# Entry of an FFN kernel: input loaded per column range into all partitions, interleaved with the first weights by quarters, norm scales applied in the split into two parts

## The chip, the cores and the metric

One core of one Trainium2 chip. The metric is the device time of one execution in microseconds (us). The kernel before was timed in three runs: 1007.42, 1010.66 and 1010.75 us, median 1010.66.

## The reference, cut to what matters

A trunk of two layers on an input x of 256 rows by 1024 columns, all float32. Each layer is `h += 0.5 * ffn(h)`, `h += mixer(h)`, `h += 0.5 * ffn(h)`; the mixer of layer 0 is a diagonal state-space layer (S5), that of layer 1 is block-sparse attention (MoBA).

```python
def rms_norm(x, g):
    y = x * lax.rsqrt(jnp.mean(x * x, axis=-1, keepdims=True) + EPS)
    return y * g

def swiglu(h, w_gate, w_up, w_down):           # h: rms_norm(h, g), 1024 columns; D_FF = 2816
    return (jax.nn.silu(h @ w_gate) * (h @ w_up)) @ w_down
```

Only the first FFN's beginning (layer 0) is touched by the change: x comes from memory, is normalised with the scales g of the first norm, and is multiplied with the gate and up weights.

## The kernel before, in words

**Phases.** `phases` is f00, s5, f01, f10, moba, f11, one after the other. The rows of h lie as two row tiles t = 0, 1 of 128 partitions each (`h2`, 128 x 2 x 1024).

**Products in two parts.** Every operand is cut into a high and a low part in the type fp32r, and a product is three matmuls (`mm3`, L385): high x high (L386), high x low weights (L387), low x high weights (L388). For a weight half of 128 x 1024, `Stream.split` (L72) lets ScalarE (ACT) copy it to whi (L81) and VectorE (DVE) subtract to wlo (L82). For x the tile `xa` holds both parts, transposed: `X["h"]` and `X["l"]`, 128 x 8 x 256, where k = 0 to 7 counts blocks of 128 columns.

**Weights.** They come in units of 1 MB in a fixed order, each with three raw buffers (RAW = 3), so the first three units are asked for when `Stream` is made. For the FFN's block j of 256 hidden columns there are two gate/up units a = 0, 1 (512 rows of w each, gate and up side by side), loaded by `ld_gu` (L161). Block 0 is loaded in steps of two k, so each of its four halves ("quarters" of the sum over 1024) is two transfers of 256 KB, one of gate and one of up. All of them are issued on SyncE's (SP) queue. `st.pump()` splits the next half if a slot is free; `st.get` splits it at the latest when it is needed. A raw buffer is asked for anew when both halves of its unit have been split.

**The order.** Every engine's instructions stand in the order in which the Python code issues them; there is no scheduler behind it. `fill` (L1304) counts estimated time and brings forward pieces of the S5 tables (the generator `tables`, L607, whose next piece is run by `next(tab, None)`) between the FFN's products.

**The entry** (L1311 to L1370):
- `ld_x(0)` (L247) loads the columns 0 to 511 of x by four transfers of 128 KB to 32 partitions each. The list `ahead` holds `ld_x(1)`, the other half, which the first call of `ld_gu` with a = 1 issues, so it stands between the second and the third pair of weight transfers.
- `busy(12)` (L1328): 12 products of `ones` with themselves, 24 matmul instructions in the profile, since a float32 product is two of them. `gains()` (L273) transposes the norm scales `gn` on TensorE (PE) and copies them to `gT`.
- `pre(t, n)` (L1311): four transposes of row tile t's columns of half n on PE (L1319), and a DVE multiply by gT in PSUM (L1320). `parts(t, n)` (L1323): ACT copies to the high part (L1325), DVE subtracts to the low part (L1326). `square` (L1339): ACT sums squares of x for the norm.
- Order: `pre` for both t of half 0, `parts` of t = 0, `busy(6)` with table pieces around it, split, `parts` of t = 1, split, two squares. `second` (L1343) does the same for half 1, and then the norm's factors on GpSimd (POOL; `rsq`, L292) and the loading of ACT's Silu table (`warm`, L226). It is a hook that runs ahead of the products q = 1, t = 0.

**gu0** (L446), the FFN's block 0: for the quarters q = 0 to 3, for t = 0, 1, two k of three matmuls, 48 in all, into the PSUM banks `psA(0)` and `psA(2)`. `hooks` holds functions to be run ahead of a pair (q, t). Then `gated` (L466) for each t: ACT computes sg, the Silu of the gate times the norm factor (L468), DVE act = up times factor times sg (L472); then `st.pump(2)`. The next block, `gu(1, 0)` (L428), has 24 matmuls for t = 0 with the transposes of act (`tr`, L474) ahead of k = 3 and k = 6. From there on the FFN goes on in this manner, with the down products between.

Of the kernel before, what the change touches and what calls it, by code (L numbers as in the profile page):

```python
# [10 lines left out]
F32 = mybir.dt.float32  # L11
F32R = mybir.dt.float32r
AF = mybir.ActivationFunctionType
OP = mybir.AluOpType
AX = mybir.AxisListType

D = 1024
# [98 lines left out]
def trunk_kernel(ctx: ExitStack, tc, x, ffn_norm, ffn_w_gate, ffn_w_up, ffn_w_down, mix_norm,  # L116
# [3 lines left out]
    nc = tc.nc  # L120
# [13 lines left out]
    def psR():  # L134
        return pp.tile([128, 512], F32, name="pR", tag="R", bufs=2)

    def psA(i):
        return pp.tile([128, 512], F32, name=f"pA{i}", tag=f"A{i}", bufs=1)
# [20 lines left out]
    ahead = []  # L159

    def ld_gu(l, i, j, a, step=4):  # L161
        def f(t):
            v = t.rearrange("p (k c) -> p k c", c=512)
            cs = slice(j * 256, (j + 1) * 256)
            if ahead and a:
                ahead.pop()()
            for k in range(0, 4, step):
                r = slice(a * 512 + k * 128, a * 512 + (k + step) * 128)
                for o, w in ((0, ffn_w_gate), (256, ffn_w_up)):
                    nc.sync.dma_start(v[:, k:k + step, o:o + 256],  # L170
                                      w[l, i, r, cs].rearrange("(k p) c -> p k c", p=128))
        return f
# [53 lines left out]
    def warm(func):  # L226

        w = sp.tile([128, 1], F32, name="warm", tag="warm", bufs=1)
        nc.scalar.activation(w, ones[:, 0:1], func)

    cst = cp.tile([128, 320], F32, name="cst")
    ident = cst[:, 0:128]
# [6 lines left out]
    h2 = cp.tile([128, 2, D], F32, name="h2")  # L239
    h = [h2[:, t, :] for t in range(2)]  # L240

    def rows(t, s, n):

        tiles = [[128 * D, 2]] if t is None else []
        return [((t or 0) * 128 + s) * D + n * 512, [[4 * D, 32]] + tiles + [[1, 512]]]

    def ld_x(n):  # L247
        for s in range(4):
            off, ap = rows(None, s, n)
            nc.sync.dma_start(h2[s * 32:s * 32 + 32, :, n * 512:(n + 1) * 512],  # L250
                              bass.AP(tensor=x.tensor, offset=x.offset + off, ap=ap))

    nc.scalar.dma_start(gn, ffn_norm.rearrange("l i (k p) -> (l i k) p", p=128))
    ld_x(0)
    warm(AF.Exp)
    ahead.append(lambda: ld_x(1))
    if "s5" in phases:
        rho = cp.tile([128, 32], F32, name="rho")
        tstack, lstack, xstack = ExitStack(), ExitStack(), ExitStack()
# [2 lines left out]
        ldt = tabp.tile([32, 2], F32, name="ldt")  # L262
# [5 lines left out]
    st = Stream(nc, units, rp, hp)  # L268

    gT = cp.tile([128, 48], F32, name="gT")  # L270
    st.gT = gT

    def gains():  # L273
        ps = psR()
        nc.tensor.transpose(ps[:, 0:32], gn, ident[0:32, 0:32])
        nc.vector.tensor_copy(gT[:, 0:32], ps[:, 0:32])
# [11 lines left out]
    X = {}  # L288
# [3 lines left out]
    def rsq(o, v, n):  # L292

        e = sp.tile([128, n], F32, name="rs_e", tag=f"rs_e{n}", bufs=2)
        nc.gpsimd.tensor_tensor(o, v, nhalf[:, 0:n], op=OP.pow)  # L295
        nc.gpsimd.tensor_tensor(e, o, o, op=OP.mult)
        nc.gpsimd.tensor_tensor(e, e, v, op=OP.mult)
        nc.gpsimd.tensor_scalar(e, e, -0.5, 1.5, op0=OP.mult, op1=OP.add)
        nc.gpsimd.tensor_tensor(o, o, e, op=OP.mult)
# [6 lines left out]
    def home(pool, ph):  # L306

        xa = pool.tile([128, 4224], F32R, name="xa")
        v = xa[:, XO[ph]:XO[ph] + 4096].rearrange("p (i k c) -> p i k c", i=2, c=256)
        return v[:, 0], v[:, 1]  # L310
# [51 lines left out]
    def boundary(nxt, parts, acc, scale, mid=None):  # L362

        if nxt is not None and nxt[0] == "f":
            order = [(0, 0), (1, 0), (0, 1), (1, 1)]
        else:
            order = [(0, 0), (0, 1), (1, 0), (1, 1)]
        for i in range(2):
            for part in parts[:-1]:
                part(*order[i])  # L370
            if mid is not None and i == 0:
                mid()
        for i, (t, n) in enumerate(order):
            for part in parts[-1:] if i < 2 else parts:
                part(t, n)
            finish(t, n, acc[2 * t + n], scale)
            if nxt is None:
                store(t, n)
            elif i:
                prep(*order[i - 1], nxt)  # L380
# [226 lines left out]
    def tables(tp):  # L607

        V, P = nc.vector, nc.gpsimd

        def T(name, *shape):
            return tp.tile([128] + list(shape), F32, name=name)
# [17 lines left out]
        for m in MPs + [TT] + t3s:  # L630
            P.memset(m, 0.0)
        yield
        dts = tp.tile([32, 2], F32, name="dts")
        nc.scalar.activation(dts, ldt, AF.Exp)
        dtb = tp.tile([32, 2, 64], F32, name="dtb")
        V.tensor_copy(dtb, dts[:, :, None].to_broadcast([32, 2, 64]))
        yield
        ps = psR()
        nc.tensor.transpose(ps[:, 0:32], scn[:, 0, :], ident[0:32, 0:32])
# [18 lines left out]
        ps = psR()  # L658
# [38 lines left out]
        q, y, y2, e0, e1, den = (T(n, 32) for n in ("q", "y", "y2", "e0", "e1", "den"))  # L697
# [213 lines left out]
        while work or later or dma:  # L911
# [8 lines left out]
            while work and work[0][1] <= now and credit >= work[0][0] and done[0] >= work[0][4]:  # L920
# [3 lines left out]
                t = max([now + LAG] + [a[0] + PACE for a in later])  # L924
# [365 lines left out]


    tab = tables(tabp) if "s5" in phases else iter(())
    next(tab, None)
    slot = [0]
# [13 lines left out]
        while extra and slot[0] > extra[0][0]:  # L1308
            extra.pop(0)[1]()

    def pre(t, n):  # L1311

        if not X:
            X[phases[0], "x"] = True
            X["h"], X["l"] = home(XP[0], phases[0])
        ps = psA(2 * t + n)
        pv = ps.rearrange("p (k c) -> p k c", c=128)
        for k in range(4):
            nc.tensor.transpose(pv[:, k, :], h[t][:, n * 512 + k * 128:n * 512 + (k + 1) * 128], ident)  # L1319
        nc.vector.tensor_tensor(pv, pv, gT[:, n * 4:n * 4 + 4, None].to_broadcast([128, 4, 128]), op=OP.mult)  # L1320
        return pv

    def parts(t, n, pv):  # L1323
        xh, xl = (X[p][:, n * 4:n * 4 + 4, t * 128:t * 128 + 128] for p in "hl")
        nc.scalar.activation(xh, pv, AF.Copy)  # L1325
        nc.vector.tensor_tensor(xl, pv, xh.bitcast(F32), op=OP.subtract)  # L1326

    def busy(n):  # L1328

        ps = psR()  # L1330
        for _ in range(n):
            mm(ps[:, 0:128], ones, ones, start=True, stop=True)

    busy(12)
    gains()
    next(tab, None)
    ss4 = sp.tile([128, 2, 2], F32, name="ss4", tag="ss4", bufs=1)

    def square(t, n):  # L1339
        sq = sp.tile([128, 512], mybir.dt.bfloat16, name="sq", tag="sq", bufs=1)  # L1340
        nc.scalar.activation(sq, h[t][:, n * 512:(n + 1) * 512], AF.Square, accum_out=ss4[:, t, n:n + 1])

    def second():  # L1343

        pv = [pre(t, 1) for t in range(2)]
        for t in range(2):
            parts(t, 1, pv[t])
        st.pump()
        for t in range(2):
            square(t, 1)  # L1350
        v2, r2 = (sp.tile([128, 2], F32, name=n, tag=n, bufs=1) for n in ("ms2", "rr2"))
        nc.gpsimd.tensor_tensor(v2, ss4[:, :, 0], ss4[:, :, 1], op=OP.add)
        nc.gpsimd.tensor_scalar(v2, v2, 1.0 / D, EPS, op0=OP.mult, op1=OP.add)
        rsq(r2, v2, 2)
        for t in range(2):
            Rr[t] = r2[:, t:t + 1]
        st.pump()
        warm(AF.Silu)

    pv = [pre(t, 0) for t in range(2)]  # L1360
    parts(0, 0, pv[0])
    next(tab, None)
    busy(6)
    st.pump()
    next(tab, None)
    parts(1, 0, pv[1])
    st.pump()
    for t in range(2):
        square(t, 0)
    first = {(1, 0): [second]}  # L1370

    for i, ph in enumerate(phases):
        nxt = phases[i + 1] if i + 1 < len(phases) else None
# [59 lines left out]
```

## Time and profile before

| | |
|---|---|
| profiled execution, device time | 1010.79 us |
| its span (first to last instruction) | 1009.0 us |
| outside the span | 1.79 us |
| mean granted clock of TensorE | 0.994 |
| bytes read from memory, written | 182.84 MB, 13.66 MB |
| DMA, mean over the span | 196 GB/s |

The profile is one execution of the program, with times in us from the span's start. In the rows of the timeline stand start, duration, engine, line and operation, then the tile written and the tiles read, the shapes, the count of instructions put together in the row ("x8"), and in brackets how long the engine sat idle before it and what ended that wait. PE is TensorE's matmuls, PEld its weight loads, SPq SyncE's queue of DMA issues. A row of the windows has, after the window's length, the busy time of PE, PEld, DVE, ACT and POOL with counts, then the granted clock of TensorE as a share of full speed, the mean busy share of the 16 DMA engines, and GB/s. A row of a DMA queue has packets, MB, and the time its packets took as a share of 16 engines' time in that window.

### The profile page before, as it was taken

How to read it: one execution, taken by the hardware profiler on the slowest of the kernel's cores; microseconds unless marked ns; L12 is line 12 of the kernel's file. 1: busy time of each engine (PE TensorE's matmuls, PEld its weight loads, DVE VectorE, ACT ScalarE, POOL GpSimd, SP SyncE). 2: the span in 40 equal slices, each digit the busy share in tenths (PEclk: the TensorE clock that was granted, in tenths of full speed). 3: DMA queues.
4: the chain of work that ended last, by engine and by line, in shares of the span. 5: the costliest groups of instructions: out<-in, count | busy, mean ns of one | idle time of the engine just before them, and what ended most of it. 6: DMA issues, size and time to landing. Idle time of an engine off the chain costs nothing.

```text
span 1009.0 us, 16573 instructions
## 1 busy us (share of the span) xinstructions
PE 996.0 (99%) x6394; PEld 892.6 (88%) x6394; DVE 704.6 (70%) x1145; ACT 574.8 (57%) x1040; POOL 165.3 (16%) x330
## 2 busy tenths in 40 slices
PE   8999999999999999999999999999999999999998
PEld 7788888888998899999989999999888899999997
DVE  4799666857968677666657766666689667766662
ACT  5566777754236556555546555553788665555551
POOL 4971222113740100000010000000342010000000
PEclk9999999999899999999999999999999999999999
DMA  8896776886736557565626765655354456656531
GB/s 249 216 295 208 253 259 210 264 317 232 260 115 189 196 186 237 167 209 168 208 85 209 236 222 170 208 168 172 116 168 139 156 174 210 221 197 206 171 125 43
DMA packets 137535, 197.59 MB, mean 196 GB/s; under 512 B 16288, under 2 KB 109040, under 8 KB 137200
## 3 DMA queue, kind: packets, MB, share of 16 engines
q1 hardware_dynamic: 133264, 183.27, 56.7%
q0 software_dynamic: 3616, 12.66, 3.2%
q8 instruction: 50, 0.82, 0.3%
q10 hardware_dynamic: 576, 0.61, 0.2%
q14 instruction: 29, 0.24, 0.1%
HBM read 182.84 MB, written 13.66 MB: 195 GB/s over the span
## 4 chain that ended last, share of the span: by engine, by line
PE 91%; DVE 3%; issue 2%; POOL 2%; ACT 1%; DMA 0%; SPq 0%; ACTq 0%; POOLq 0%; DVEq 0%
PE pM L541 12%; PE pM L540 12%; PE pM L542 12%; PE pA L387 9%; PE pA L386 9%; PE pA L388 9%; PE pM L386 5%; PE pM L387 5%; PE pM L388 5%; PE pR L322 1%; DVE wlo L82 1%; POOL qrs L295 1%; PE pR L872 1%; PE pR L1035 1%; PE pR L1034 1%
## 5 line engine op out<-in xcount | busy, mean ns | idle before, releaser
L540 PE MATMUL pM<-xa,whi 128*128 128x256 f32 x1056 | 295.7, 280 | 0.0
L541 PE MATMUL pM<-xa,whi 128*128 128x256 f32 x1056 | 294.9, 279 | 0.0
L542 PE MATMUL pM<-xa,wlo 128*128 128x256 f32 x1056 | 294.7, 279 | 0.0
L88 DVE SCALAR_TENSOR_TENSOR wlo<-raw,gT,whi 128x512 fp32r<-128x512 f32 x328 | 228.0, 748 | 70.2 <-ACT whi L87 70.0
L82 DVE TENSOR_TENSOR wlo<-raw,whi 128x1024 fp32r<-128x1024 f32 x156 | 190.7, 1237 | 55.2 <-ACT whi L81 54.0
L87 ACT ACTIVATE whi<-raw,gT 128x512 fp32r<-128x512 f32 x328 | 213.5, 711 | 19.2 <-PE pA L388 14.1
L541 PEld LDWEIGHTS pM<-xa,whi 128*128 128x128 f32 x1056 | 198.5, 188 | 2.6
L540 PEld LDWEIGHTS pM<-xa,whi 128*128 128x128 f32 x1056 | 198.5, 188 | 2.3
L542 PEld LDWEIGHTS pM<-xa,wlo 128*128 128x128 f32 x1056 | 198.5, 188 | 0.0
L81 ACT ACTIVATE whi<-raw 128x1024 fp32r<-128x1024 f32 x156 | 160.8, 1054 | 21.9 <-PE pM L541 6.3
L386 PE MATMUL pA<-whi,ah 128*128 128x512 f32 x352 | 138.8, 394 | 0.0
L387 PE MATMUL pA<-wlo,ah 128*128 128x512 f32 x352 | 137.7, 391 | 0.0
L388 PE MATMUL pA<-whi,al 128*128 128x512 f32 x352 | 137.7, 391 | 0.0
L555 ACT ACTIVATE sg<-gr 128x256 f32<-128x256 f32 x66 | 27.6, 418 | 165.5 <-DVE gr L552 165.5
L386 PE MATMUL pM<-whi,xa 128*128 128x512 f32 x288 | 120.0, 417 | 1.5 <-ACT whi L81 1.5
L387 PE MATMUL pM<-wlo,xa 128*128 128x512 f32 x288 | 113.5, 394 | 0.9 <-DVE wlo L82 0.9
L388 PE MATMUL pM<-whi,xa 128*128 128x512 f32 x288 | 113.5, 394 | 0.0
L337 POOL TENSOR_TENSOR ms<-ss 128x1 f32<-128x1 f32 x10 | 1.9, 194 | 475.9 <-ACT sq L334 475.9
L388 PEld LDWEIGHTS pA<-whi,al 128*128 128x128 f32 x352 | 66.1, 188 | 14.4
L386 PEld LDWEIGHTS pA<-whi,ah 128*128 128x128 f32 x352 | 66.2, 188 | 11.6
L387 PEld LDWEIGHTS pA<-wlo,ah 128*128 128x128 f32 x352 | 66.2, 188 | 11.3
L552 DVE TENSOR_TENSOR gr<-pM,rrow 128x512 f32<-128x512 f32 x66 | 45.5, 689 | 40.6 <-PE pM L542 40.4
(253 smaller groups left out, 1289.6 us busy)
## 6 DMA issues: line engine op xcount, KB each, us to landing
raw<-in_ffn_w_down_dram SPq DMA_DIRECT2D x44, 1024.0 KB, 5.5
raw<-in_ffn_w_gate_dram SPq DMA_DIRECT2D x80, 512.0 KB, 4.0
raw<-in_ffn_w_up_dram SPq DMA_DIRECT2D x80, 512.0 KB, 5.1
raw<-in_moba_w_qkv_dram SPq DMA_DIRECT2D x12, 1024.0 KB, 5.2
TB<-dB SPq DMA_DIRECT2D x8, 768.0 KB, 5.9
raw<-in_ffn_w_gate_dram SPq DMA_DIRECT2D x16, 256.0 KB, 4.4
raw<-in_ffn_w_up_dram SPq DMA_DIRECT2D x16, 256.0 KB, 4.6
dB<-tt POOLq DMA_DIRECT2D x16, 256.0 KB, 5.2
```

The source lines that it names most:

```text
L81: nc.scalar.activation(hi, r, AF.Copy)
L82: nc.vector.tensor_tensor(lo, r, hi.bitcast(F32), op=OP.subtract)
L87: nc.scalar.activation(hi[:, c], r[:, c], AF.Identity, scale=g)
L88: nc.vector.scalar_tensor_tensor(lo[:, c], r[:, c], g, hi[:, c].bitcast(F32), op0=OP.mult, op1=OP.subtract)
L386: mm(o, xh, wh, start=start, stop=False)
L387: mm(o, xh, wl, start=False, stop=False)
L388: mm(o, xl, wh, start=False, stop=stop)
L540: mm(o, a, xh, start=k == 0 and i == 0, stop=False, skip_group_check=True)
L541: mm(o, a, xl, start=False, stop=False, skip_group_check=True)
L542: mm(o, b, xh, start=False, stop=k == 7, skip_group_check=True)
L552: V.tensor_tensor(gr, ps.rearrange("p (i c) -> p i c", i=2), Rr["row"][:, None, :].to_broadcast([128, 2, 256]), op=OP.mult)
L555: nc.scalar.activation(sg, gr[:, 0, :], AF.Silu)
```

## The change

- **Transfers of x.** `ld_x(c, n)` loads n columns from column c by two transfers, one for each row tile, each to all 128 partitions. The source's access pattern is 4 runs of 32 rows (`[[D, 4], [4 * D, 32], [1, n]]`), where before's was 32 rows, then 2 tiles, then the columns; partition 32s + i holds row 4i + s as before. x comes in three pieces: columns 0 to 255, 256 to 511 and 512 to 1023.
- **Interleaving.** `ld_gu` now takes the next entry of `ahead` at each step of two k. SP's order is: x's first quarter, first weights, x's second quarter, second weights, x's half, third weights, fourth weights.
- **Scales in the parts.** `quarter(q)` takes the place of `pre` and `parts`: four transposes (two k, both t) into one PSUM bank (1 or 3), and for each k an ACT operation 128x256 that multiplies by gT while it writes the high part, and a DVE operation that multiplies and subtracts for the low part. The DVE multiplies in PSUM go. In the built program the second ACT operation of a quarter waits for the first DVE operation.
- **Order.** `busy(8)` and `busy(3)` in place of 12 and 6. Each quarter has a hook of its own; the third quarter's transposes stand on PE ahead of the second quarter's 12 products, as the hook (1, 0) holds them, and the fourth's ahead of the third's. The norm's factors and the Silu table come in hook (2, 0). The hooks (3, 0) and (3, 1) each split one more half, so the first unit of block 1 is split before the sg.
- **Tables.** The exponential `dtb` is one ACT operation that reads its input broadcast; before, ACT wrote `dts` and DVE copied it to `dtb` (L636).

```diff
@@ ld_gu
-            if ahead and a:
-                ahead.pop()()
             for k in range(0, 4, step):
+                if ahead:
+                    ahead.pop(0)()
@@ ld_x
-    def ld_x(n):
-        for s in range(4):
-            off, ap = rows(None, s, n)
-            nc.sync.dma_start(h2[s * 32:s * 32 + 32, :, n * 512:(n + 1) * 512],
-                              bass.AP(tensor=x.tensor, offset=x.offset + off, ap=ap))
+    def ld_x(c, n):
+        for t in range(2):
+            nc.sync.dma_start(h2[:, t, c:c + n],
+                              bass.AP(tensor=x.tensor, offset=x.offset + t * 128 * D + c,
+                                      ap=[[D, 4], [4 * D, 32], [1, n]]))
...
-    ld_x(0)
+    ld_x(0, 256)
     warm(AF.Exp)
-    ahead.append(lambda: ld_x(1))
+    ahead.extend([lambda: None, lambda: ld_x(256, 256), lambda: ld_x(512, 512)])
@@ tables
-        dts = tp.tile([32, 2], F32, name="dts")
-        nc.scalar.activation(dts, ldt, AF.Exp)
         dtb = tp.tile([32, 2, 64], F32, name="dtb")
-        V.tensor_copy(dtb, dts[:, :, None].to_broadcast([32, 2, 64]))
+        nc.scalar.activation(dtb, ldt[:, :, None].to_broadcast([32, 2, 64]), AF.Exp)
@@ entry
-    def pre(t, n):
...
-    def parts(t, n, pv):
...
+    def quarter(q):
...
+        ps = psA(1 + 2 * (q % 2))
+        pv = ps.rearrange("p (k c) -> p k c", c=256)
+        for k in range(2):
+            for t in range(2):
+                c = (2 * q + k) * 128
+                nc.tensor.transpose(pv[:, k, t * 128:(t + 1) * 128], h[t][:, c:c + 128], ident)
+        for k in range(2):
+            g = gT[:, 2 * q + k:2 * q + k + 1]
+            xh, xl = (X[p][:, 2 * q + k, :] for p in "hl")
+            nc.scalar.activation(xh, pv[:, k, :], AF.Identity, scale=g)
+            nc.vector.scalar_tensor_tensor(xl, pv[:, k, :], g, xh.bitcast(F32), op0=OP.mult, op1=OP.subtract)
...
-    def second():
...
+    def factors():
...
+    busy(8)
+    gains()
     next(tab, None)
+    quarter(0)
+    busy(3)
     st.pump()
-    next(tab, None)
-    parts(1, 0, pv[1])
-    st.pump()
-    for t in range(2):
-        square(t, 0)
-    first = {(1, 0): [second]}
+    square(0, 0)
+    first = {(0, 1): [lambda: next(tab, None), st.pump, lambda: quarter(1), lambda: square(1, 0)],
+             (1, 0): [lambda: next(tab, None), lambda: quarter(2), st.pump, lambda: square(0, 1)],
+             (2, 0): [lambda: quarter(3), st.pump, lambda: square(1, 1), factors],
+             (3, 0): [st.pump], (3, 1): [st.pump]}
```

More of the change, by code (lines that the diff above doesn't have):

```diff
@@ L1315, in pre @@
             X["h"], X["l"] = home(XP[0], phases[0])
[L1316 to L1321, printed above, removed]
-    def parts(t, n, pv):
-        xh, xl = (X[p][:, n * 4:n * 4 + 4, t * 128:t * 128 + 128] for p in "hl")
-        nc.scalar.activation(xh, pv, AF.Copy)
-        nc.vector.tensor_tensor(xl, pv, xh.bitcast(F32), op=OP.subtract)
+        ps = psA(1 + 2 * (q % 2))
[9 more added lines that the diff above has]
+            nc.vector.scalar_tensor_tensor(xl, pv[:, k, :], g, xh.bitcast(F32), op0=OP.mult, op1=OP.subtract)
     def busy(n):
@@ L1332, in busy @@
             mm(ps[:, 0:128], ones, ones, start=True, stop=True)
-    busy(12)
-    gains()
-    next(tab, None)
     ss4 = sp.tile([128, 2, 2], F32, name="ss4", tag="ss4", bufs=1)
@@ L1341, in square @@
         nc.scalar.activation(sq, h[t][:, n * 512:(n + 1) * 512], AF.Square, accum_out=ss4[:, t, n:n + 1])
-    def second():
-        pv = [pre(t, 1) for t in range(2)]
-        for t in range(2):
-            parts(t, 1, pv[t])
-        st.pump()
-        for t in range(2):
-            square(t, 1)
+    def factors():
         v2, r2 = (sp.tile([128, 2], F32, name=n, tag=n, bufs=1) for n in ("ms2", "rr2"))
@@ L1356, in second @@
             Rr[t] = r2[:, t:t + 1]
-        st.pump()
         warm(AF.Silu)
-    pv = [pre(t, 0) for t in range(2)]
-    parts(0, 0, pv[0])
+    busy(8)
+    gains()
     next(tab, None)
-    busy(6)
+    quarter(0)
+    busy(3)
     st.pump()
-    next(tab, None)
-    parts(1, 0, pv[1])
-    st.pump()
-    for t in range(2):
-        square(t, 0)
-    first = {(1, 0): [second]}
+    square(0, 0)
[3 more added lines that the diff above has]
+             (3, 0): [st.pump], (3, 1): [st.pump]}
     for i, ph in enumerate(phases):
```

## The prediction

> **What bounds the kernel now.** I read the page first (busy times, then the chain that ended last), then the timeline of the first 36 us, where the whole change lies, then windows of the same time for the clock, and last the DMA views.
>
> ```profile
> span 1009.0 us, 16573 instructions
> PE 996.0 (99%) x6394; PEld 892.6 (88%) x6394; DVE 704.6 (70%) x1145; ACT 574.8 (57%) x1040; POOL 165.3 (16%) x330
> PE 91%; DVE 3%; issue 2%; POOL 2%; ACT 1%; DMA 0%; SPq 0%; ACTq 0%; POOLq 0%; DVEq 0%
> ```
>
> PE is busy for 99% and has 91% of the chain. After the entry little is to be had, and what the change earns must be a wait or slow clock of PE at the start. The timeline of the entry:
>
> ```profile
> 0.98 5.49 PE L1332 MATMUL pR<-ones 128*128 128x128 f32 x24 [0.98 <-POOL ones L224]
> 6.40 0.31 PE L275 MATMUL pR<-cst,gn 32*128 32x32 f32 x1
> 6.64 1.28 PE L1319 MATMUL pA<-cst,h 128*128 128x128 f32 x8
> 7.52 1.44 DVE L1320 TENSOR_TENSOR pA<-pA,gT 128x512 f32<-128x512 f32 x2
> 8.40 0.60 ACT L1325 ACTIVATE xa<-pA 128x512 fp32r<-128x512 f32 x1 [3.60 <-DVE pA L1320]
> 8.90 1.05 ACT L81 ACTIVATE whi<-raw 128x1024 fp32r<-128x1024 f32 x1
> 9.03 0.69 DVE L1326 TENSOR_TENSOR xa<-pA,xa 128x512 fp32r<-128x512 f32 x1
> 10.00 0.49 PE L386 MATMUL pA<-whi,xa 128*128 128x512 f32 x1 [0.24 <-DVE gm L646]
> 10.03 1.22 DVE L82 TENSOR_TENSOR wlo<-raw,whi 128x1024 fp32r<-128x1024 f32 x1
> 11.31 0.50 PE L387 MATMUL pA<-wlo,xa 128*128 128x512 f32 x1 [0.82 <-DVE wlo L82]
> ```
>
> The order is: warm-up products, scales, transposes of x, multiply, high part, then the weights' whi and wlo. The first product that matters is the second one, at 11.31, when wlo is there. 48 products make gu0; the last begins at 24.29. What follows it is the other loss:
>
> ```profile
> 24.29 0.40 PE L388 MATMUL pA<-whi,xa 128*128 128x512 f32 x1
> 24.73 0.48 ACT L468 ACTIVATE sg<-pA,rr 128x256 f32<-128x256 f32 x1 [0.84 <-PE pA L388]
> 25.10 2.94 ACT L81 ACTIVATE whi<-raw 128x1024 fp32r<-128x1024 f32 x3
> 25.24 0.48 DVE L472 SCALAR_TENSOR_TENSOR act<-pA,rr,sg 128x256 f32<-128x256 f32 x1 [0.83 <-ACT sg L468]
> 26.20 0.50 PE L386 MATMUL pM<-whi,xa 128*128 128x512 f32 x1 [1.51 <-ACT whi L81]
> 27.46 0.74 PE L387 MATMUL pM<-wlo,xa 128*128 128x512 f32 x1 [0.76 <-DVE wlo L82]
> 28.43 0.63 PE L386 MATMUL pM<-whi,xa 128*128 128x512 f32 x1
> 28.85 0.63 PE L387 MATMUL pM<-wlo,xa 128*128 128x512 f32 x1
> 34.84 0.39 PE L387 MATMUL pM<-wlo,xa 128*128 128x512 f32 x1
> 35.07 0.39 PE L388 MATMUL pM<-whi,xa 128*128 128x512 f32 x1
> ```
>
> gu(1,0) waits 1.51 for whi and 0.76 for wlo, since nobody splits its weights before the two sg. Then its products stand 0.42 apart (28.43, 28.85), where later ones stand 0.23 apart (34.84, 35.07). The windows tell why:
>
> ```profile
> 24.37:27.78 3.41, 1.14 (x4) 0.51 (x3) 2.12 (x4) 3.05 (x4) 2.90 (x7) 0.97 0.98 207
> 27.79:31.20 3.41, 3.41 (x11) 2.54 (x10) 2.03 (x2) 0.25 (x1) 3.04 (x5) 0.54 0.31 72
> 31.20:34.61 3.41, 3.25 (x16) 2.43 (x15) 2.27 (x3) 2.66 (x4) 3.00 (x6) 1.00 0.89 255
> 35.10:110.00 74.90, 74.90 (x361) 61.06 (x360) 66.72 (x100) 46.67 (x72) 39.23 (x74) 1.00 0.84 258
> ```
>
> The columns are PE, PEld, DVE, ACT and POOL busy, then the granted clock. In a 3.41-us stretch PE was busy 1.14 us, and the next stretch ran at a clock of 0.54. Such a stretch delays work by half its length, 1.7 us. From 35.1 on PE is busy without a gap. So I measure the change by when gu(1,0)'s last product begins: 35.07 now, 10.8 after gu0's last.
>
> **The change, part by part.** *The new chain per quarter of x.* A quarter has 4 transposes, then ACT high, DVE low, ACT high, DVE low; in the built order the second high stands behind the first low, so these run one after the other. The nearest rows for a 128x256 piece are the sg (0.48) and act (0.48) above, the bounds half of the 128x512 rows (0.30 and 0.35) and those rows whole (0.60 and 0.69); I take 0.48, the same shape. The first weights are split behind the second high: 4 transposes 0.64 (half of 1.28), three pieces 1.45, whi 1.05, wlo 1.22, with 0.1 for handing over: 4.4 us from x's first quarter to the second product. Gone are the DVE multiplies, 0.72 each (1.44/2).
>
> *Fewer warm-up products* (8 in place of 12): 24 instructions take 5.49, 16 take 3.66, so PE comes to the scales at 4.64 and not at 6.40. The 3 in place of 6 further on stand ahead of products that wait for whi anyway; cost nothing either way. The merged dtb saves DVE a piece beside x's chain, worth nothing on PE.
>
> *Two more splits ahead.* The hooks (3,0) and (3,1) pump gu(1,0)'s first two halves while gu0's last quarter runs. Then 1.51 + 0.76 of wait go, and with them the slow stretch. What is late next is the second unit's halves, whose whi must stand behind the two sg: 0.96 and 1.05, and wlo behind the two act, until 3.2 us after gu0's last; 12 products are 12 x 0.227 = 2.7 of that, so 0.5 remains as a wait, and the last half costs 0.3 to 0.6 more. 24 products are 5.45, two pairs of transposes (tr) 0.3: with those waits **6.8** in place of 10.8.
>
> *Squares and factors* are spread over the hooks. The rows of before:
>
> ```profile
> 17.38 0.62 ACT L1341 ACTIVATE sq<-h 128x512 bf16<-128x512 f32 x1
> ...
> 18.92 0.19 POOL L1352 TENSOR_TENSOR ms<-ss 128x2 f32<-128x2 f32 x1 [10.94 <-ACT sq L1341]
> ...
> 19.81 1.28 ACT L229 ACT_TABLE_LOAD   x1
> ...
> 21.74 0.20 POOL L299 TENSOR_TENSOR rr<-rr,rs_e 128x2 f32<-128x2 f32 x1
> ```
>
> Four squares as before, but the last one, the table load (1.28, with 0.2 for the warm-up behind it) and POOL's 3.0 us (18.92 to 21.94) now come in hook (2,0), behind the fourth weights' whi and ahead of the first extra split. They are covered by the 24 products of gu0's second half (5.45), as long as those aren't early; if that cover is gone, the first sg waits for POOL and gu(1,0)'s first wlo for the table, 0.4 us by the times below, which lies inside the waits counted above.
>
> *SP* issues two transfers less before the fourth weights (6 of x for 8, 0.42 each), and the first weights stand behind two x transfers, not four; they aren't on the path, as whi's row names no DMA. From 35 us on the b and c tables' loads go one place later among the weights, beside a queue with time to spare; nothing.
>
> *The transfers.* These decide. The DMA view of x's line, then of three windows (weights in 1-KB packets, 1.8 us; a later phase's 2-KB packets, 1.8 us; x beside other transfers, 2.6 us):
>
> ```profile
> L250 SPq DMA_DIRECT2D h<-in_x_dram x8: 378/425/467, 0.7 to 6.0; - x8
> ...
> DMA to landing us min/median/max: 2.6/4.9/6.8
> ```
>
> ```profile
> q1 hardware_dynamic: 576, 0.61, 103.7%
> ```
>
> ```profile
> q1 hardware_dynamic: 312, 0.61, 87.1%
> ```
>
> ```profile
> q1 hardware_dynamic: 344, 0.53, 71.6%
> ```
>
> MB over window, 16 engines and share give 20.4, 24.3 and 17.8 GB/s for one engine. The first x landed at 0.73 + 2.6 = 3.33; at 16 engines its 128 KB take 0.4, so bytes begin at 2.94.
>
> The new x transfers name 4 runs of 32 rows in their source; before's named 32, the weights 128, and all these kept 16 engines busy. No row has a transfer with an outermost 4. Bounds: it is spread like the others (x at 326 GB/s), or by its outermost count over 4 engines, 4 x 20.4 = 82 GB/s in 1-KB packets and 4 x 24.3 = 97 GB/s in 2-KB ones. I take the second, since the outermost count is just what the rows that used 16 engines do not share with it, and keep both ends.
>
> The Trainium skill, DMA: Bandwidth & Descriptors, section "Why a DMA increments its semaphore by 16 and not by 1", speaks against the change: a transfer runs on the largest number of engines up to 16 that divides the slowest dimension of both its patterns, which is 4 here. Before's rows agree for 32 and 128, and none shows a 4. By it the sum is 1011.0, without it 1008.0 (below).
>
> By 4 engines: 128 KB take 1.6, 256 KB 2.7, and 256 KB of weights on all engines 0.8. One queue in its order gives: x's first quarter 6.1, first weights 7.6, second quarter 10.8, second weights 12.3, x's half 17.7, third weights 19.3, fourth 20.8. Then, by the pieces above:
> - second product 6.1 + 4.3 = 10.4 (now 11.31), and t = 0's others at half clock, since PE had little to do for four us: 12.5. Then the tables' and second quarter's transposes and t = 1's six products, to 15.7.
> - Third quarter's transposes are queued on PE ahead of second quarter's 12 products, and all of these wait for x's half: 2 us, to 18.0. Transposes 0.6, products 2.7: 21.3.
> - whi of the third weights begins behind x's high parts at 20.1; wlo ends at 22.4. So third quarter's second product is at 22.5, and its end at 25.0. The fourth likewise: its transposes run at 21.3, four pieces to 24, wlo 25.8, its end **28.5**, against 24.5 now: +4.0.
> - gu(1,0) 6.8 in place of 10.8: -4.0.
>
> Sum: 0. If a slow stretch falls in the 2-us wait it costs 0 to 1.7, of which wlo's 22.4 and 25.8, which PE's clock does not move, hide most: +0.2. On the profiled execution's 1010.79 (span 1009.0 and 1.79 around it), which lies 0.13 above the median, **1011.0**. Own range 1009 to 1013.5: 6.8 could be 5.8 and the hand-overs 0.8 shorter; the slow stretch could cost its full 1.7 and x's half come 1 us later.
>
> *After 35 us* PE, DVE, ACT and POOL do the same in the same order, with splits up to one place ahead until about 45 us. Two splits less for DVE in a stretch where it is busy 66.72 of 74.90 can only help; I count nothing.
>
> **The rivals.**
> - *x's transfers are spread over all 16 engines.* For it: every transfer seen here is. Against it: the outermost 4. x's first quarter lands with the scales at 4.3; scales' transpose and copy to 5.1, then 4.4: second product 9.5, 1.8 sooner. But PE, whose warm-up now ends at 4.64, stands mostly idle to 9.4, so that a slow stretch follows (1.7), and gu0 ends at about 24.5 as now. Then 6.8 in place of 10.8: -4.0. I let DVE's little room behind it (8.2 us in 75) eat 1.2, as the splits that were ahead are used up: **1008.0**, 1006 to 1009.5.
> - *Slower: x's packets move at the third window's 17.8 GB/s, on 4 engines.* For it: that row is x's own. Against it: few x packets in it had company for long. Then 71 GB/s: 1.85 and 3.7 a transfer and 1.6 for a pair of weights. x's half lands at 2.94 + 3.7 + 1.6 + 3.7 + 1.6 + 7.4 = 20.9, 3.2 later, and the rest moves with it; the wait on PE, now 5 us, surely brings a slow stretch, 1.7: 1011.0 + 3.2 + 1.7 = **1015.9**. It decides once x's half lands after 20, where the wait is longer than a 3.41-us stretch.
> - That the change doesn't do what it says is the forecast itself: all 128 partitions are reached, through a quarter of the engines.
>
> **How the numbers follow.** Forecast 0.52, 16 engines 0.34, slower 0.12; 0.02 for less than 1005.6 by a luckier clock. The runs shown differ by 3.3 (1007.42 to 1010.75), about what one slow stretch or two make, and each case's range holds that. From 1006.0 to 1014.5 lie all but the tails and the slower rival. About 0.5% (5 us) is what a measurement of this kernel can tell from no change: faster (below 1005.6) 0.06, the 0.02 and the lower tail of 16 engines; slower (above 1015.7) 0.07, half the slower rival and the forecast's tail; same 0.87.
>
> **What would show it.** In the changed profile: x's line from issue to landing (the half at about 17.7, or before 12); the mean DMA share while x moves (near 0.3 with 4 engines, near 1 with 16); a wait of PE in L387 or the transposes ending at x's half; second product at 10.4 or 9.5; gu0's last at 28.3 or 24.4; no wait for whi after it; gu(1,0)'s last at 35.1 or 31.3. The forecast is wrong if the half lands late without a later end of gu0, or if gu(1,0) takes far from 6.8.

## The result, and the profile after

The changed kernel takes **1020.08 us** (median of 4 runs, 1017.18 to 1025.85) against 1010.70 beside it: ratio 1.011, 95% interval 1.0082 to 1.0138. It is slower by about 1%, above the range of 1009 to 1013.5. The profiled execution took 1022.31, 11.5 more than that of before. Its page (span, busy time of each engine, chain by engine, chain by line):

```profile
span 1020.5 us, 16539 instructions
PE 1000.8 (98%) x6380; PEld 894.8 (88%) x6380; DVE 702.3 (69%) x1144; ACT 576.4 (56%) x1044; POOL 164.8 (16%) x330
PE 84%; POOL 5%; DVE 4%; issue 3%; DMA 2%; ACT 1%; SPq 0%; POOLq 0%; DVEq 0%; ACTq 0%
PE pM L541 12%; PE pM L542 12%; PE pM L543 12%; PE pA L387 9%; PE pA L389 9%; PE pA L388 9%; PE pM L387 4%; PE pM L389 4%; PE pM L388 4%; DMA h<-in_x_dram 2%; DVE wlo L82 1%; PE pR L323 1%; POOL qrs L296 1%; PE pR L871 1%; PE pR L1033 1%
```

PE is busy for 4.8 us more (1000.8 for 996.0), part of the 11.5; the rest is waiting. Two things weigh more in the chain than before: x's transfer with 2% (0% before), and POOL with 5% (2% before). What PE waited for in the first 50 us (total, times, longest), and the timeline's rows around it:

```profile
PE pA L1320 <- DMA h<-in_x_dram: 4.1, 2, 2.2
PE pA L387 <- ACT whi L81: 1.3, 1, 1.3
PE pR L1331 <- POOL ones L224: 1.0, 1, 1.0
PE pA L388 <- DVE wlo L82: 1.0, 2, 0.5
PE pM L388 <- DVE wlo L82: 0.6, 1, 0.6
```

```profile
7.53 0.90 PE L1320 MATMUL pA<-cst,h 128*128 128x128 f32 x3 [1.90 <-DMA h<-in_x_dram]
...
12.23 0.80 PE L388 MATMUL pA<-wlo,xa 128*128 128x512 f32 x1 [0.46 <-DVE wlo L82]
...
20.39 0.78 PE L1320 MATMUL pA<-cst,h 128*128 128x128 f32 x3 [2.16 <-DMA h<-in_x_dram]
...
31.95 0.39 PE L389 MATMUL pA<-whi,xa 128*128 128x512 f32 x1
...
39.39 0.39 PE L389 MATMUL pM<-whi,xa 128*128 128x512 f32 x1
```

x's first quarter was there at 7.5, its half at 20.4. gu0's last product begins at 31.95 (24.29 before), gu(1,0)'s last at 39.39 (35.07). So the entry alone is 4.3 late, not 11.5. The next 6 are lost where nothing was expected, between 56 and 82 us:

```profile
61.80 0.44 PE L486 MATMUL pR<-cst,act 128*128 128x128 f32 x2 [1.02 <-DVE act L473]
77.30 0.63 PE L811 MATMUL pR<-cst,cn 128*64 128x128 f32 x4 [2.95 <-DVE al L489]
```

```profile
74.00:77.30 3.30, 0.36 (x2) 0.00 (x0) 3.30 (x7) 0.19 (x1) 3.30 (x7) 1.00 0.52 151
77.30:80.70 3.40, 3.40 (x13) 2.55 (x13) 2.50 (x5) 0.75 (x2) 2.61 (x7) 0.69 1.04 357
80.70:84.10 3.40, 3.40 (x13) 2.58 (x13) 2.06 (x4) 1.90 (x2) 0.00 (x0) 0.81 0.60 252
```

In the windows (PE, PEld, DVE, ACT, POOL busy, then clock) VectorE is busy for the whole 3.30 us in which PE does 0.36, and then PE's clock is 0.69 and 0.81. Upstream of it stand two rows of the timeline:

```profile
28.91 0.62 POOL L1341 TENSOR_TENSOR ms<-ss 128x2 f32<-128x2 f32 x1 [20.94 <-ACT sq L1337]
```

```profile
55.54 0.23 DVE L677 COPY e<-c 128x16 f32<-128x16 f32 x1 [2.44 <-POOL c L668]
```

The same two ends of that wait in before, POOL's c and VectorE's reading of it:

```profile
42.40 0.22 POOL L669 TENSOR_SCALAR c<-e 128x32 f32<-128x32 f32 x1
46.60 0.19 DVE L678 COPY e<-c 128x16 f32<-128x16 f32 x1
```

POOL begins the norm's factors at 28.91, where it began at 18.92. Its table chain stands behind them in its order. Its result c comes at 55.3, 12.9 us later than before (42.4), and VectorE stands 2.44 us for it. Ten of the 12.9 are the later start; the other 2.9 come up under e4.

The same products (by their number in the FFN's first phase and after it) in each profiled execution: how much later (+) or earlier (-) they begin than in before. This table is worked out from the timelines, one execution each:

| kernel | gu0's last (24.29) | gu(1,0)'s last (35.07) | at 254.55 | at 321.60 |
|---|---|---|---|---|
| changed | +7.65 | +4.31 | +10.34 | +11.88 |
| e1, 128 rows | +0.97 | -2.33 | +3.82 | +0.69 |
| e2, 8 runs | +2.43 | -0.88 | +3.71 | +2.10 |
| e3, x alone | +7.03 | +6.98 | +7.00 | +7.01 |
| e4, splits alone | -0.05 | -4.88 | -3.31 | -3.44 |
| e5, four of 32 | +0.84 | -2.49 | +3.59 | +0.44 |
| e6, factors early | +8.55 | +3.81 | +7.67 | +7.59 |
| e7, e5 and table later | +1.66 | -1.64 | -0.28 | -1.31 |
| e8, e4 and table later | -0.04 | -4.85 | -4.82 | -4.84 |
| e9, changed and table later | +6.57 | +3.27 | +6.31 | +8.65 |
| e10, as e4 | -0.05 | -4.89 | -3.72 | -3.68 |
| e11, as e8 | -0.07 | -4.91 | -4.81 | -6.41 |
| e12, e8 and dtb | -1.11 | -5.95 | -5.65 | -8.78 |

So the changed kernel's 11.5 is 4.3 by the end of gu(1,0), 6.0 more by 254 us, and the rest behind that. Of the 6.0, 1.4 is the stretch at half clock that follows the wait of 2.95 (its lag grows from 8.9 at 77.7 to 10.3 at 81.8). In e2 no such stretch follows its waits, and its loss there is 4.6.

The last column has a second thing in it. In the s5 phase PE stops near 270 us in every kernel, for 1.1 us in most (1.7 in e7, 2.5 in e9). Here are the wait's row in before, then the windows of before, then those of e12:

```profile
PE pR L1033 <- issue: 1.1, 1, 1.1
```

```profile
266.48:269.89 3.41, 2.31 (x22) 2.10 (x21) 3.41 (x9) 1.81 (x6) 2.13 (x3) 1.00 1.04 398
271.40:274.80 3.40, 3.40 (x18) 3.40 (x18) 3.22 (x5) 0.05 (x1) 2.04 (x4) 0.50 0.29 82
274.80:278.20 3.40, 3.40 (x23) 3.40 (x23) 2.48 (x5) 1.58 (x3) 3.32 (x3) 0.72 0.67 228
```

```profile
262.00:266.00 4.00, 2.89 (x27) 2.68 (x26) 3.96 (x11) 0.66 (x2) 2.64 (x3) 1.00 0.97 379
266.00:270.00 4.00, 4.00 (x37) 4.00 (x36) 4.00 (x8) 1.64 (x3) 2.72 (x3) 1.00 0.72 257
```

Before ran at 0.50 behind the stop in this execution, e12 at full clock. That is 3 us between two executions and has nothing to do with the change, so the column at 254.55 is the fair one for an entry, and medians can be off by 1 to 3.

### The profile page after: what moved, and what is told of

Same layout as the page of the kernel before. It is cut to its first block, busy times and chain, and to the rows that moved or that the text cites. A ratio compares the mean times of both kernels' runs of the same rounds, so it can differ in the third digit from the quotient of the medians.

```text
span 1020.5 us, 16539 instructions
## 1 busy us (share of the span) xinstructions
PE 1000.8 (98%) x6380; PEld 894.8 (88%) x6380; DVE 702.3 (69%) x1144; ACT 576.4 (56%) x1044; POOL 164.8 (16%) x330
## 4 chain that ended last, share of the span: by engine, by line
PE 84%; POOL 5%; DVE 4%; issue 3%; DMA 2%; ACT 1%; SPq 0%; POOLq 0%; DVEq 0%; ACTq 0%
PE pM L541 12%; PE pM L542 12%; PE pM L543 12%; PE pA L387 9%; PE pA L389 9%; PE pA L388 9%; PE pM L387 4%; PE pM L389 4%; PE pM L388 4%; DMA h<-in_x_dram 2%; DVE wlo L82 1%; PE pR L323 1%; POOL qrs L296 1%; PE pR L871 1%; PE pR L1033 1%
```

## The experiments

Two theories. **A, the width**: x runs on 4 engines, and the rest follows. **B, the order**: the new order makes POOL's chain late, whatever the transfers do.

**e1: 128 rows named first.** The rows of x land in other partitions, so the sequence that is computed is a permuted one.

```diff
-                                      ap=[[D, 4], [4 * D, 32], [1, n]]))
+                                      ap=[[D, 128], [1, n]]))
```

> The changed kernel with one edit: the source of each x transfer names 128 single rows, not 4 runs of 32 (so rows land in other partitions, and the rows of the output are those of a permuted sequence; the number and size of all operations stay). Theory A, the width: x runs on 4 engines and all loss follows from that. Then x's half lands before 13, gu0's last product begins at 24 to 25 (31.95 now, 24.29 before the change), no wait behind 40 us, POOL's norm chain starts before 22 (28.91 now), time 1006 to 1009. Theory B, the order: the loss comes from POOL's chain and PE's transposes behind later hooks, whatever the transfers do. Then POOL starts at 25 or later, the wait near 77 us stays, time 1014 or more.

Measured: 1011.72 (ratio to before 1.0033, 1.0011 to 1.0055), between the two theories' times. gu0's last product begins at 25.27 (+0.97), just above A's 24 to 25. But the waits behind 40 us stayed, as B had it:

```profile
PE pR L811 <- DVE al L489: 3.0, 1, 3.0
PE pR L486 <- DVE act L473: 1.0, 1, 1.0
```

POOL starts at 22.24 here, where A had it before 22 and B at 25 or later. So both theories hold a part: A is worth 6.7 us by gu0's end, and about 6 us are lost behind gu(1,0) with either width (6.1 here by 76 us).

**e2: 8 runs of 16 rows.**

```diff
-                                      ap=[[D, 4], [4 * D, 32], [1, n]]))
+                                      ap=[[D, 8], [8 * D, 16], [1, n]]))
```

> The same with 8 runs of 16 rows (rows permuted again). If the outermost count is the number of engines, x moves at twice the changed kernel's rate (about 195 GB/s while x alone moves, DMA share near 0.5), x's half lands at 14 to 16, gu0 ends at 25 to 28, time 1008 to 1013. If the count doesn't matter: as the changed kernel, 1020, or as the variant with 128 rows.

Measured: 1012.40 (1.0035, 1.0019 to 1.0050), within the expected time; x's half lands at 16.7, a little late for 14 to 16. The DMA views of a stretch in which only the engines that carry x are busy, in the changed kernel (10 to 11.2 us) and in e2 (5.6 to 6.4, weights among its packets), and of e1 at the changed kernel's place:

```profile
DMA packets 116, 0.12 MB, mean 96 GB/s; under 512 B 3, under 2 KB 116, under 8 KB 116
q1 hardware_dynamic: 116, 0.12, 27.3%
```

```profile
DMA packets 155, 0.14 MB, mean 171 GB/s; under 512 B 23, under 2 KB 155, under 8 KB 155
q1 hardware_dynamic: 136, 0.13, 51.6%
```

```profile
q1 hardware_dynamic: 458, 0.44, 108.8%
```

A share of 27% of 16 engines is 4 of them, 52% is 8, and all 16 work with 128 rows. The trace also records when each engine reports the end of its part of a transfer: for a transfer of x 4 engines do in the changed kernel, 8 in e2 and 16 in e1. The outermost count is the number of engines. The rule of the Trainium skill, DMA: Bandwidth & Descriptors, section "Why a DMA increments its semaphore by 16 and not by 1" (the largest number up to 16 that divides the slowest dimension of both patterns), gives 4, 8 and 16 here, and the three shares agree. With 8 engines the rest of the chain hides most of the slower transfers: gu0 ends 1.5 behind e1.

**e3: x alone, in the kernel before.**

```diff
-        for s in range(4):
-            off, ap = rows(None, s, n)
-            nc.sync.dma_start(h2[s * 32:s * 32 + 32, :, n * 512:(n + 1) * 512],
-                              bass.AP(tensor=x.tensor, offset=x.offset + off, ap=ap))
+        for t in range(2):
+            nc.sync.dma_start(h2[:, t, n * 512:(n + 1) * 512],
+                              bass.AP(tensor=x.tensor, offset=x.offset + t * 128 * D + n * 512,
+                                      ap=[[D, 4], [4 * D, 32], [1, 512]]))
```

> The kernel before with one edit: each half of x by two transfers of 4 runs of 32 rows. Theory A: x's first half lands at about 8 (5.86), its second at about 17 (12.79); gu0 ends 3 to 5 later than 24.29, POOL's norm chain starts as much later, time 1013 to 1018. Theory B: within 2 us of before.

Measured: 1016.16 (1.0057, 1.0042 to 1.0072), within A's range. But the delay by gu0's end is 7.0, not 3 to 5: x's halves land later than expected, at 10.9 and 20.9 by the products that wait for them. The loss goes with one row of the waits, and nothing is added behind 40 us:

```profile
PE pA L1319 <- DMA h<-in_x_dram: 7.4, 3, 3.0
```

Here POOL's chain is 6 us late (its first factor starts at 25.46, 18.92 before; c at 48.5, 42.4 before) and PE 7, so nobody waits for POOL.

**e4: the two earlier splits alone, in the kernel before.**

```diff
-    first = {(1, 0): [second]}
+    first = {(1, 0): [second], (3, 0): [st.pump], (3, 1): [st.pump]}
```

> The kernel before with one edit: hooks (3, 0) and (3, 1) each split one half more. My forecast's term: gu(1,0) takes 6 to 7 us in place of 10.8, no stretch at half clock, time 1007 (3 to 4 less than before), if nothing is given back. Rival: VectorE is so full from 35 to 110 us that the gain comes back as a wait for wlo or act there: within 1 us of before.

Measured: 1004.55 (0.9960, 0.9944 to 0.9975); once more as e10:

> The kernel before with the two earlier splits, once more, beside the next one on the same chip: 1004 to 1006.

1005.15 (0.9960, 0.9945 to 0.9975). The first and last product of gu(1,0) follow at once on gu0's last (24.25):

```profile
24.47 0.39 PE L386 MATMUL pM<-whi,xa 128*128 128x512 f32 x1
...
30.19 0.39 PE L388 MATMUL pM<-whi,xa 128*128 128x512 f32 x1
```

5.9 us, where it was 10.8: the best part of the change, worth 4.9. Of it 1.6 is lost by 254 us (1.2 in e10), behind a wait of VectorE for POOL's c (4.2 us).

POOL starts its factors at 18.91 here, as before, and yet c comes at 46.0, 3.6 later. The same operation of POOL in before, and in e4 beside a split on VectorE:

```profile
22.96 0.22 POOL L669 TENSOR_SCALAR q<-aim 128x32 f32<-128x32 f32 x1
```

```profile
23.92 1.24 POOL L669 TENSOR_SCALAR q<-aim 128x32 f32<-128x32 f32 x1
23.92 1.16 DVE L82 TENSOR_TENSOR wlo<-raw,whi 128x1024 fp32r<-128x1024 f32 x1
```

From the factors to c POOL has 48 operations. In before 8 of them take over 0.9 us, in e4 12, and each of these overlaps a wlo split of VectorE; those that overlap none take at most 0.4. So the two earlier splits are themselves a reason why c is late. The changed kernel has 12 such operations too, and e3, without the earlier splits, has 8.

**e5: four transfers of 32 partitions in the changed kernel**, which gives the right rows and 16 engines.

```diff
-        for t in range(2):
-            nc.sync.dma_start(h2[:, t, c:c + n],
-                              bass.AP(tensor=x.tensor, offset=x.offset + t * 128 * D + c,
-                                      ap=[[D, 4], [4 * D, 32], [1, n]]))
+        for s in range(4):
+            nc.sync.dma_start(h2[s * 32:s * 32 + 32, :, c:c + n],
+                              bass.AP(tensor=x.tensor, offset=x.offset + s * D + c,
+                                      ap=[[4 * D, 32], [128 * D, 2], [1, n]]))
```

> The changed kernel with one edit: each piece of x comes by four transfers of 32 partitions (both row tiles in each, 32 rows named first), as the kernel before had them. If the outermost count is what matters, as the variant with 128 rows: gu0's last product begins at about 25.3, 1010 to 1013. If 128 partitions in one transfer matter beside it (SP issues 12 transfers for 6), x's second quarter and half land 1 to 2 us later and it is 1012 to 1014.

Measured: 1013.93 (1.0045, 1.0025 to 1.0065), above the 1010 to 1013 of the first case and in the 1012 to 1014 of the second. But its ten runs lie between 1010.35 and 1017.68, e1's between 1010.66 and 1018.42, so the medians tell little. x's half lands at 12.4, 1.8 later than in e1, as the second case had it, and yet the entry is e1's within 0.2 us: whether a transfer reaches 32 or 128 partitions makes no difference to gu0's end. gu(1,0) ends 2.5 ahead of the kernel before's, where e4's is 4.9 ahead. So the rest of the change, its new order and shorter warm-up, costs 2.4 at the entry even with 16 engines. In e1 PE waits 1.56 for the first whi and 0.77 for wlo, and its clock is 0.50 from 10.0 to 13.4, a slow stretch that the 16-engine rival had foreseen.

**e6: factors early, in the changed kernel.**

```diff
-             (1, 0): [lambda: next(tab, None), lambda: quarter(2), st.pump, lambda: square(0, 1)],
-             (2, 0): [lambda: quarter(3), st.pump, lambda: square(1, 1), factors],
+             (1, 0): [lambda: next(tab, None), lambda: quarter(2), lambda: square(0, 1), lambda: square(1, 1), factors, st.pump],
+             (2, 0): [lambda: quarter(3), st.pump, lambda: warm(AF.Silu)],
```

(`warm(AF.Silu)` leaves `factors`.)

> The changed kernel (x by 4 engines) with one edit: the squares of x's second half and the norm's factors on POOL stand in hook (1, 0), ahead of the third weights' split; only the Silu table stays in hook (2, 0). Theory POOL: the wait near 77 us comes from POOL's table chain, which begins behind the factors (28.9). POOL then starts at 23 to 25, VectorE's wait for the table's c (2.4 us at 55) goes, and the time is 1014 to 1016. Rival, VectorE too full: 1019 to 1021, as changed. By either, the third weights' whi is 1.6 us later.

Measured: 1017.19 (1.0079, 1.0061 to 1.0096), between the two theories' numbers. POOL starts at 25.14, VectorE's wait for c is gone, and the loss behind gu(1,0) is 3.9 in place of 6.0. No stretch at half clock follows here, which is 1.4 of this gain, so the waits themselves are only 0.7 less:

```profile
PE pR L811 <- DVE al L489: 1.7, 1, 1.7
PE pR L486 <- DVE act L473: 0.5, 1, 0.5
```

**e7: e5 with VectorE's table work planned later.**

```diff
-LOADS, C_AT, E_AT, ... = (...), 44, 26, 36, 0.46, 12, 4.0, 8.0
+LOADS, C_AT, E_AT, ... = (...), 44, 32, 36, 0.46, 12, 4.0, 8.0
```

> The variant with four transfers of 32 partitions, and VectorE's first table work (which reads POOL's c) planned 6 later in the estimated time (E_AT 32 for 26). Theory POOL: VectorE splits weights while POOL ends, no wait of PE at 60 to 80 us, 6 less than the variant without: 1005 to 1007. Rival, VectorE too full: the wait only moves, within 2 us of that variant.

Measured: 1010.66 (1.0011, 0.9999 to 1.0022). The median fell by 3, not 6; in the profiled execution the loss between gu(1,0) and 254 us fell from 6.1 to 1.4 (1.5 of that is the stretch at half clock, at 71.6 us in e5 and gone here), and one wait is left:

```profile
PE pR L810 <- DVE al L488: 1.2, 1, 1.2
```

**e8 and e11: e4 with the table work 4 later** (E_AT 30).

> The kernel before with the two earlier splits, and E_AT 30 for 26. The kernel with the splits alone lost 1.6 of its 4.9 us between 50 and 72 us, behind a 4.2-us wait of VectorE for POOL's c. Theory POOL: that 1.6 comes back, 1003. Rival: 1004.5, the same as with the splits alone.

> The same with E_AT 30. By the entry alone 1.5 less than the splits alone; the medians so far (1005.6 and 1004.6) had it the other way, which I put down to the half-clock stretch that follows the 1.1-us stop of PE in the s5 phase near 270 us and is there in some executions and not in others. If so it is 0 to 2 less on one chip, with its spread.

Measured: 1005.60 (0.9962, 0.9947 to 0.9977) and 1005.74 (0.9960, 0.9944 to 0.9975). At 254 us it keeps all 4.8, 1.5 more than e4, with no wait of PE between 24 and 130 us. The medians don't show that: e4's 1004.55 and e10's 1005.15 are level with them, and the stretch near 270 us is larger than the difference. In these profiles the later table work takes the loss away; a gain in the median isn't shown, and e11's expectation of 0 to 2 less than e10 was missed by 0.6.

**e9: the changed kernel with the table work 6 later.**

> The changed kernel itself (x by 4 engines), with VectorE's first table work planned 6 later (E_AT 32 for 26). The changed kernel lost 6.1 us between 56 and 82 us. If that loss is VectorE standing for POOL's c, it falls to 1 to 2, and the time is 1015 to 1016 (1020 as changed). If VectorE is behind because its weights landed late, the loss stays: 1019 to 1021.

Measured: 1018.20 (1.0083, 1.0060 to 1.0106). The loss between gu(1,0) and 254 us is 3.0 in place of 6.0. VectorE's wait for c is gone and with it half of the loss, of which 1.4 is the stretch at half clock that doesn't follow here. In place of the wait for c VectorE waits longer for whi, 10.6 us against 7.0 (28 to 100 us, total, times, longest):

```profile
DVE wlo L82 <- ACT whi L81: 10.6, 9, 2.7
```

Neither theory alone gives this number.

**e12: e8 with dtb by one ACT operation.**

> The same as the one before, with dtb by one ACT operation as in the changed kernel. VectorE's copy of 0.93 stood ahead of its first multiply by the scales, so x's parts come up to 0.4 earlier: 0 to 0.4 less than without.

Measured: 1004.85 (0.9956, 0.9941 to 0.9971), the lowest ratio, but within the intervals of e4, e8, e10 and e11. In the profiled execution x's chain begins earlier by more than expected: products 1.1 earlier, not 0.4. Its transposes begin at 5.97 and x's first high part at 7.37; in e4 the transposes are nearly as early (6.11), and the high part stands at 8.39.

## Why the prediction was wrong, point by point

- **x on 4 engines** was right, and so was its rate with the other engines idle: 96 GB/s, 82 to 97 forecast. The chain per quarter was right too: its pieces took 0.47 and 0.48 (0.48 forecast), and from x's first quarter at 7.53 to the second product at 12.23 it is 4.7 (4.4).
- **"One queue in its order gives: x's first quarter 6.1 ... x's half 17.7"** failed in its rates, not in its order. The trace's records of when each engine has ended its part take it apart. For each transfer of weights, twelve engines are done early and four late, and the late ones keep the order of issue with x:

| piece | forecast | the four engines of x done | the other twelve done |
|---|---|---|---|
| x's first quarter | 6.1 | 7.49 | |
| first weights | 7.6 | 9.11 | 7.47 |
| x's second quarter | 10.8 | 11.80 | |
| second weights | 12.3 | 13.49 | 10.27 |
| x's half | 17.7 | 20.35 | |
| third weights | 19.3 | 21.57 | 14.25 |

  x's second quarter, with the twelve all but idle (a share of 27% above), took 2.7 us: 24 GB/s for each of the four. x's half, while the twelve moved weights, took 6.9 where 5.4 was forecast: 19 GB/s each, not 24.3. The first quarter's second transfer took 2.7, not 1.6, also beside weights on the others. So the term that was too small is x's time beside weights; why an engine is slower there no run took apart.
- **"If a slow stretch falls in the 2-us wait it costs 0 to 1.7, ... hide most"** failed with it. The wait came later, and the clock behind it was half:

```profile
17.00:20.40 3.40, 1.24 (x7) 0.74 (x5) 0.74 (x2) 1.32 (x5) 0.00 (x0) 1.00 0.93 261
20.40:23.80 3.40, 3.40 (x10) 2.82 (x11) 1.08 (x3) 2.04 (x4) 0.00 (x0) 0.52 0.90 252
```

  Together the term of +4.0 for gu0's end measured +7.65. The third quarter's transposes begin 2.4 later than forecast (20.39 for 18.0); the other 1.3 come behind them, with the products 0.43 apart in the slow stretch. The slower rival had this much of it: 17.8 GB/s an engine, x's half after 20, and a surely slow stretch.
- **"gu(1,0) 6.8 in place of 10.8"** was right in kind: 7.4 in the changed kernel (so -3.3 where -4.0 was forecast), 5.9 in e4.
- **"After 35 us ... I count nothing"** is the step that failed most: 6.0 us. The order of instructions is nearly the same there, but the engines no longer stood equally late. POOL began 10 late, the earlier splits on VectorE made its chain 2.9 longer, and PE was 4.3 late. In before c was there at 42.6 and VectorE read it at 46.6, so 4 us of slack lay between them, and the shift used it up. VectorE, busy for 23.6 of the 26 us from 56 to 82, passed its delay on to PE with a half-clock stretch on top. e6, e7 and e9 take the wait for POOL away and get back 2.1, 4.7 and 3.0, of which 1.4 to 1.5 each is that stretch. With 16 engines (e7) this is most of the loss. What makes up the rest of it with x on 4 engines (ACT's waits for late weights are a guess) was not taken apart.
- **"covered by the 24 products of gu0's second half"**, said of the factors, looked only at the first sg (which did wait, 0.39), and not at what else is queued on POOL behind them.
- **"The merged dtb ... worth nothing on PE"** holds for the changed kernel as far as is known, where the first product waits for x; in the kernel before it was worth about 1 us (e12).
- **The rival with 16 engines** (1008.0) comes out at 1011.72 in e1: its entry was right within 0.8 us at gu0's end (+0.97 for +0.2), gu(1,0) took 7.5 for 6.8, and of the 6.1 us lost behind it 1.2 were forecast.

## What to carry to other kernels

A transfer that reaches all partitions can still run on a quarter of the engines: look at the count of the outermost dimension of both patterns, and at the mean DMA share while it moves alone. Price it by what its engines do while the others are busy, not by their best rate. When a part of the work is moved to a later place, follow every engine's queue behind it to the next point where two engines meet, since a slack of 4 us there is easily used up by a shift of 10 on one engine and 4 on the other. And test the parts of a bundle alone: this one held a gain of about 5 us (two splits of weights earlier) under the losses of the slow transfers, of the new order at the entry and of the late POOL chain.

## What the runs showed of the hardware

- While x's transfers were on 4 engines, SP took 0.53 to 1.89 us to issue one of them (0.38 to 0.47 before) and up to 2.69 for one of weights behind them, and the view has no landing for x's:

```profile
L250 SPq DMA_DIRECT2D h<-in_x_dram x6: 534/626/1893, 0.7 to 7.5; - x6
```

- From the factors to c POOL's operations took 0.2 to 0.4 us in before and e4 where VectorE ran no wlo split, and many of those beside one took 1.0 to 1.4 (22.96 in before and 23.92 in e4, shown there).
- TensorE's clock fell to half behind stretches that were not idle: 1.24 of 3.40 us busy from 17.0, and 2.31 of 3.41 up to 269.9, with no single wait over 2.16 and 1.10. A stop of 1.1 us was enough in some executions and not in others, which makes 3 us of spread in a kernel of 1010. The Trainium skill, TensorE: Matmul & The Clock Gate, section "Part 1: The HAM clock gate", speaks of at least one idle window of about 3.4 us; these rows, and the 1.14 of 3.41 in before, have work in the window and still the half clock behind it.
- The clock column can't be relied on ahead of a trace's first clock record (17.15 in the changed kernel). The window says 1.00, and yet the products stand 0.43 apart, as they do at 0.50, and not 0.23:

```profile
13.60:17.00 3.40, 3.40 (x13) 2.42 (x12) 1.78 (x5) 1.50 (x2) 0.00 (x0) 1.00 0.78 209
```

```profile
13.67 0.63 PE L388 MATMUL pA<-wlo,xa 128*128 128x512 f32 x1
14.10 0.63 PE L389 MATMUL pA<-whi,xa 128*128 128x512 f32 x1
```
